# An encoder block on one core: the end of w_out's written TensorE order, and its last T4 product between two banks of transposes

## The chip, the cores and the metric

The kernel runs on one core of one Trainium2 chip. The metric is the device time of one execution in microseconds (us). Before the change the median of three runs is 1320.53 us (1319.11 to 1321.21).

## The reference

One layer of a streaming encoder, 1024 tokens of width 1024, all in float32:

```
def reference(x, norm_mix_pre, norm_mix_post, w_in, b_f, conv_w, w_branch, w_out,
              norm_ffn_pre, norm_ffn_post, w_gate_up, w_down):
    for l in range(DEPTH):
        h = rmsnorm(x, norm_mix_pre[l])
        m = mixer(h, w_in[l], b_f[l], conv_w[l], w_branch[l], w_out[l])
        x = x + rmsnorm(m, norm_mix_post[l])
        h = rmsnorm(x, norm_ffn_pre[l])
        f = swiglu(h, w_gate_up[l], w_down[l])
        x = x + rmsnorm(f, norm_ffn_post[l])
    return x
```

The mixer projects `h` with w_in, runs a gated short convolution and a causal attention with forget gates side by side, takes each through its branch matrix, merges the two under sigmoid gates and multiplies by w_out (1024 x 1024). `swiglu` multiplies by w_gate_up (1024 x 5632), forms silu(g) * u, and multiplies by w_down (2816 x 1024). The change lies at the seam between w_out and gate_up: the last product of the mixer, its norm and residual, the norm before the feed-forward part, and the first products of gate_up.

## The kernel before

**Arithmetic.** Every float32 operand is split into a high and a low part in a reduced float32 type: ScalarE copies the high part (`copy`), VectorE subtracts it (`split`, line 132). A product is three matmuls for each block of the contraction, high x high, high x low, low x high (`mm3`, line 137). The large matrix products use the Strassen-Winograd scheme: seven block products instead of eight, named by their operands, A11, A12, A22, S1 to S4 on one side and B11, B21, B22, T1 to T4 on the other. Here "the T4 product" is A22 with T4. `prod` (line 617) is one block product: four blocks of the contraction, 12 matmuls, into one bank of PSUM.

**w_out.** The 1024 tokens are eight tiles of 128 rows, taken as four pairs (`PAIRS`). For pair i the output has four blocks. The steps, at lines 1656 to 1711, are these. `first` and `second` are A11 and A12. `p_s2` and `p_s1` are S2 and S1. `p_s3` accumulates S3 into the bank that held S2's sum (`b1s[i]`); then ScalarE copies that bank to `c22s[i]` and VectorE adds S1's bank (`b3s[i]`), both raised in priority by `ahead`. `p_s4` accumulates S4 into `b3s[i]`, so it comes after that add; VectorE adds the result to `keeps[i]` and ScalarE squares it for the norm. `p_a22` accumulates the T4 product into `b1s[i]`, so it comes after the copy; ScalarE squares the result. `e_norm(i)` (line 1713) takes the sums of squares of both, scales the pair's two rows of tiles, adds the residual x, stores the sum, squares it, and scales it by the next norm. The first tile of the pair lands in `keeps[i]` (a `raw` buffer of the weights for the first three pairs), the second in `tt`, a tag with one buffer, so the second tile of pair i + 1 waits until that of pair i has been transposed.

**Transposes.** `e_turn(i, tiles)` (line 1740) turns tile 2i + e on TensorE: eight 128 x 128 transposes in two banks of four, q = 0 and 1. The bank q = 0 is copied by ScalarE into rows 0 to 3 of `um`, the bank q = 1 into rows 4 to 7; the copies are raised in priority. `half_split(B11, i)` (line 1796) splits rows 0 to 3 of a pair's columns, `half_split(B21, i)` rows 4 to 7; these are the moving operands of gate_up's A11 and A12 products for the first 512 tokens. `h2_sums(sl)` (line 1800) forms T1 to T4 from tiles sl and 4 + sl: eight subtractions on VectorE and four high parts on ScalarE.

**PSUM.** In this stage pool `pk` has four banks, one for each pair's `b1s` and then for gate_up's first four sums, and pool `psm3` four, for S1/S4 sums (`b3s`), transposes and A12 sums of w_out. From line 1867 on one pool of eight takes their place.

**gate_up's first products.** Before the main loop over blocks of the hidden width, A11 (`f_begin`, line 1774) and A12 (`f_end`, line 1783) of the first eleven blocks are done, as they need only tokens 0 to 511. `f_begin(n)` loads and splits the weights (SyncE's queue, three `raw` buffers, four `hi`, three `lo`), multiplies, and ScalarE copies the sum away; `f_end(n)` accumulates A12 into the same bank, so it waits for that copy. Results go to memory by GpSimd's queue. The first four (`begin_early`, `end_early`) stand between the transposes of pairs 2 and 3, the others follow with `h2_sums`.

**What sets the order.** A planner orders the instructions of each engine by priority (earlier in the program first) and its own costs. An engine named in `strict[0]` is not planned: each instruction is tied behind the one that was written before it on that engine (lines 67 to 82). `pinned(call, name)` (line 119) does this for the instructions of one call. `ahead` raises the priority of a call. Each engine then works off its order strictly: an item that waits holds up all behind it. In this stage `strict[0] = ("tensor",)` holds from line 1814 to line 1862, so TensorE's order is as written; ScalarE's and VectorE's are planned. For the last pair (i = 3) TensorE's written order is: S1, S3, both banks of tile 0 of pair 1, S4, both banks of tile 1 of pair 1, T4; and then `begin_early(0)`, `begin_early(1)`, `end_early(0)`, the transposes of pair 2, and so on.

Of the kernel before, what the change touches and what calls it, by code (L numbers as in the profile page):

```python
# [47 lines left out]
def block_kernel(  # L48
# [18 lines left out]
    strict = [()]  # L67
# [42 lines left out]
    def add(o, a, b):  # L110
        nc.vector.tensor_tensor(o, a, b, op=ALU.add)
# [7 lines left out]
    def pinned(call, *names):  # L119

        was, strict[0] = strict[0], names
        call()
        strict[0] = was

    def ahead(call, by=80):
        with tc.high_priority(offset=by):
            call()

    def copy(o, a):
        nc.scalar.activation(o, a, AF.Copy)  # L130
# [404 lines left out]
    def flat(t):  # L535
        return t.rearrange("p a b -> p (a b)")
# [7 lines left out]
    def raw_t():  # L544
        return wtile("raw", 3)
# [7 lines left out]
    def s4_t():  # L553
        return wtile("s4", 1, F32, (P, 4, P))
# [62 lines left out]
    def prod(ps, w, b, first):  # L617
        (ah, al), (bh, bl) = w, b
        kw = {} if first else dict(skip_group_check=True)
        for k in range(4):  # L620
            mm3(
                ps,
                (ah[:, k, :], al[:, k, :]),
                (bh[:, k, :], bl[:, k, :]),
                first and k == 0,
                k == 3,
                **kw,
            )
# [812 lines left out]
    def x_tile(n, p=None):  # L1441
        if n == 3:
            p, tag = yb_pool, "yb"
        else:
            p, tag = p or wx, f"x{n}"
        return p.tile([P, 2, 4, NC], F32R, tag=tag, name=f"x{n}", bufs=1)

    def both(t):
        return t[:, 0], t[:, 1]
# [183 lines left out]
    def square(src, acc):  # L1633
        junk = ep.tile([P, NC], F32, tag="junk", name="junk")
        nc.scalar.activation(junk, src, AF.Square, accum_out=acc)
# [33 lines left out]
    def rest_ops(i):  # L1669
        a = slice(2 * i * P, (2 * i + 1) * P)  # L1670
        b = slice((2 * i + 1) * P, (2 * i + 2) * P)
        hx, lx = hi_t(), lo_t()
        split(hx[:, LO], lx[:, LO], um[:, LO, a])
        h1, l1 = hi_t(), lo_t()
        split(h1, l1, um[:, :, b])
        split(hx[:, UP], lx[:, UP], s3[i])
        h4, l4 = s4h_t(), s4l_t()
        split(h4, l4, um[:, UP, a])
        return dict(
            S2=(hx[:, LO], lx[:, LO]), S3=(hx[:, UP], lx[:, UP]),  # L1680
            S1=(h1[:, LO], l1[:, LO]), A22=(h1[:, UP], l1[:, UP]),
            S4=(h4, l4),
        )

    def p_s2(i):
        prod(b1s[i], rests[i]["S2"], wob[T2], False)
        copy(keeps[i][:, n2], b1s[i])

    def p_s1(i):
        b3s[i] = bank(psm, "b3")  # L1690
        prod(b3s[i], rests[i]["S1"], wob[T1], True)

    def p_s3(i):
        prod(b1s[i], rests[i]["S3"], wob[T3], False)
        c22s[i] = t_(fe, "c22")

        def keep():
            copy(c22s[i], b1s[i])
            add(c22s[i], c22s[i], b3s[i])

        ahead(keep)
        square(c22s[i], qbs[i][:, 1:2])

    def p_s4(i):
        prod(b3s[i], rests[i]["S4"], wob[B22], False)
        add(keeps[i][:, n2], keeps[i][:, n2], b3s[i])
        square(keeps[i][:, n2], qbs[i][:, 0:1])

    def p_a22(i):
        prod(b1s[i], rests[i]["A22"], wob[T4], False)  # L1710
        square(b1s[i], qas[i][:, 1:2])

    def e_norm(i):
        qa = qas[i]
        add(qa, qa, qbs[i])
        rs = scale2(qa)
        tt = keeps[i], ep.tile([P, D], F32, tag="t", name="tt", bufs=1)
        xp = [xts.popleft() for _ in range(2)]
        ssq = st2("ssq")
        for e, parts in enumerate(  # L1720
            (((slice(0, D), keeps[i]),), ((n1, b1s[i]), (n2, c22s[i])))
        ):
            for ns, c in parts:
                nc.vector.scalar_tensor_tensor(
                    tt[e][:, ns], c, rs[:, e : e + 1], gpo[:, ns], op0=ALU.mult, op1=ALU.mult
                )
            add(xp[e], xp[e], tt[e])
            rows_ = slice((2 * i + e) * P, (2 * i + e + 1) * P)
            nc.gpsimd.dma_start(x2_dram[rows_, :], xp[e])
            nc.scalar.activation(tt[e], xp[e], AF.Square, accum_out=ssq[:, e : e + 1])  # L1730
        rs = scale2(ssq)
        for e in range(2):
            nc.vector.scalar_tensor_tensor(
                tt[e], xp[e], rs[:, e : e + 1], gpr, op0=ALU.mult, op1=ALU.mult
            )
            if 2 * i + 3 + e < ST:
                xts.append(load_xt(2 * i + 3 + e))
        turned.append(tt)

    def e_turn(i, tiles=(0, 1)):  # L1740
        for e in tiles:
            st = 2 * i + e
            ss = slice(st * P, (st + 1) * P)
            for q in range(2):
                tp = psm.tile([P, 4, P], F32, tag="mm", name="tp")

                def turns():
                    for k in range(4):
                        kt = 4 * q + k
                        nc.tensor.transpose(  # L1750
                            tp[:, k, :], turned[i][e][:, kt * P : (kt + 1) * P], ident
                        )

                pinned(turns, "tensor")
                ahead(lambda: copy(um[:, 4 * q : 4 * q + 4, ss], tp))
# [18 lines left out]
    def f_begin(n, b1, p1):  # L1774
        f = FIRSTS[n]
        w, _ = prep_first(f_src(f)[0])
        prod(b1, w["A11"], hb[B11], True)
        pinned(lambda: copy(p1, b1), *(("scalar",) if n >= 8 else ()))
        if f > 1:
            nc.gpsimd.dma_start(pre_dram[f][0], p1)  # L1780
        begun[n] = w, b1, p1

    def f_end(n, c11):
        f = FIRSTS[n]
        w, b1, p1 = begun.pop(n)
        prod(b1, w["A12"], hb[B21], False)
        copy(c11, b1)
        if f > 1:
            nc.gpsimd.dma_start(pre_dram[f][1], c11)
        else:  # L1790
            kept[f] = p1, c11
# [4 lines left out]
    def half_split(b, i):  # L1796
        ss = slice(2 * i * P, (2 * i + 2) * P)
        split(hb[b][0][:, :, ss], hb[b][1][:, :, ss], um[:, (LO, UP)[b], ss])
# [18 lines left out]
    for i in range(PAIRS):  # L1817
        if i + 1 < PAIRS:
            rests.append(rest_ops(i + 1))
        if i:  # L1820
            p_s1(i)
        p_s3(i)
        if i > 1:
            e_turn(i - 2, (0,))
        if i + 1 < PAIRS:
            p_s2(i + 1)
        if i == 3:
            p_s4(i)
        if i > 1:
            e_turn(i - 2, (1,))  # L1830
            half_split(B11, i - 2)
        if i == 2:
            hb.append(both(x_tile(2)))
        if i > 1:
            half_split(B21, i - 2)
        for p_ in ((p_a22, p_s4), (p_s4, p_a22), (p_s4, p_a22), (p_a22,))[i]:
            p_(i)
        e_norm(i)
    hb.append(None)
# [4 lines left out]
    def begin_early(f):  # L1844
        if f == 2:
            raw_t()
        f_begin(f, pk.tile([P, NC], F32, tag="p1", name="b1"), early[f])

    def end_early(f):
        f_end(f, flat(s4_t()))  # L1850

    begin_early(0)
    begin_early(1)
    end_early(0)
    e_turn(2)
    begin_early(2)
    end_early(1)
    begin_early(3)
    end_early(2)
    e_turn(3)  # L1860
    end_early(3)
    strict[0] = ()
    ep_close()
    fe_close()
    psm_close()
# [533 lines left out]
```

## Time and profile before

| | |
|---|---|
| median of 3 runs | 1320.53 us (1319.11 to 1321.21) |
| the profiled execution | 1322.75 us, of which the span from the first to the last instruction is 1321.0 |
| mean granted TensorE clock | 0.997 |
| matmuls, on TensorE | 6776 |
| w_out's first bank of transposes in this stage | starts at 649.17 us |
| gate_up's first product | starts at 675.40 us |

A profile shows one execution. Its page gives busy times by engine and the chain of work that ended last; the views of the trace list, for each engine, the instructions in order of time, merged where they are alike, with the idle time ahead of them in brackets and what ended it. All operations go through helpers, so each has the line 77, and groups are told apart by the names of their tiles: `tp` is a bank of transposes, `raw`, `tt` and `keep` the tiles that they turn, `um` where they land, `x` the operands that `half_split` and `h2_sums` write (and w_out's weights before that), `c` the c22 and c21 tiles, `p` a bank of pool `pk` that w_out uses, `b` any other sum, `s` and `sx` room for gate_up's first results.

### The profile page before, as it was taken

To read this page: it belongs to the slowest core of one execution; us is meant where nothing else is said; L and a number is where in the kernel's file an instruction comes from. 1 tells how busy PE (TensorE), PEld (TensorE's weight loads), DVE (VectorE), ACT (ScalarE), POOL (GpSimd) and SP (SyncE) were. 2 spreads that over 40 slices of the span, in tenths; PEclk is the share of its full clock that TensorE was granted. 3 is DMA by queue.
4 is the path that set the end of the run, shared out by engine and by line. 5 is a ranking of instruction groups with operands and counts; after the bars stand their busy time and mean duration, and the time that the engine had idled before them with its cause. 6 is when DMAs were issued, how large, how long until landed. Compare 5 with 4: busy or idle time off the path is not lost.

```text
span 1321.0 us, 18315 instructions
## 1 busy us (share of the span) xinstructions
PE 1303.3 (99%) x6776; PEld 1089.5 (82%) x6776; DVE 1015.3 (77%) x1595; ACT 583.6 (44%) x935; POOL 154.9 (12%) x289
## 2 busy tenths in 40 slices
PE   9999999999999999999989999999999999999997
PEld 8988888887888888888877888888888888888886
DVE  6975979875656877587888688898888887676685
ACT  6642333253355866445666422323333334444452
POOL 0001100021012212020011012121001110000000
PEclk9999999999999999999999999999999999999999
DMA  6347757778646444499365545563223337966541
GB/s 223 110 117 223 201 155 209 192 212 228 175 144 200 161 145 151 158 344 360 112 214 167 161 160 179 171 200 104 80 96 121 104 106 275 329 254 193 158 167 64
DMA packets 207242, 235.15 MB, mean 178 GB/s; under 512 B 12064, under 2 KB 150368, under 8 KB 207152
## 3 DMA queue, kind: packets, MB, share of 16 engines
q1 hardware_dynamic: 159136, 156.08, 37.5%
q0 software_dynamic: 18832, 63.22, 13.1%
q10 hardware_dynamic: 29184, 14.68, 4.4%
q8 instruction: 53, 0.87, 0.3%
q14 instruction: 37, 0.30, 0.1%
HBM read 161.79 MB, written 72.16 MB: 177 GB/s over the span
## 4 chain that ended last, share of the span: by engine, by line
PE 92%; DVE 3%; DMA 2%; ACT 2%; issue 1%; SPq 0%; POOL 0%; DVEq 0%; ACTq 0%; POOLq 0%
PE b L77 53%; PE pd L77 16%; PE pba L77 3%; PE p L77 3%; PE pv L77 3%; PE tps L77 3%; PE po L77 3%; PE sp L77 2%; PE pbp L77 2%; PE pbv L77 1%; PE zb L77 1%; PE ma L77 1%; PE q L77 1%; PE tp L77 1%; PE mb L77 1%
## 5 line engine op out<-in xcount | busy, mean ns | idle before, releaser
L77 PE MATMUL b<-x,hi 128*128 128x512 f32 x1088 | 338.3, 392 | 4.9 <-ACT c L77 2.9
L77 PEld LDWEIGHTS b<-x,hi 128*128 128x128 f32 x1088 | 204.8, 189 | 48.4 <-ACT c L77 3.3
L77 PE MATMUL b<-x,lo 128*128 128x512 f32 x544 | 213.0, 392 | 0.0
L77 DVE TENSOR_TENSOR lo<-raw,hi 128x1024 fp32r<-128x1024 f32 x90 | 108.3, 1204 | 64.6 <-PE b L77 57.6
L77 ACT ACTIVATE hi<-raw 128x1024 fp32r<-128x1024 f32 (+1 forms) x96 | 97.6, 1018 | 103.7 <-PE b L77 55.2
L77 PEld LDWEIGHTS b<-x,lo 128*128 128x128 f32 x544 | 102.8, 189 | 22.0 <-DVE lo L77 0.3
L77 DVE TENSOR_TENSOR c<-c,b 128x512 f32<-128x512 f32 x138 | 93.7, 680 | 21.6 <-PE b L77 13.4
L77 ACT ACTIVATE hi<-sx 128x1024 fp32r<-128x1024 f32 (+1 forms) x42 | 43.8, 1042 | 125.4 <-PE b L77 116.5
L77 DVE TENSOR_TENSOR lo<-sx,hi 128x1024 fp32r<-128x1024 f32 (+1 forms) x42 | 50.3, 1197 | 25.4 <-PE b L77 22.6
L77 DVE TENSOR_TENSOR sx<-raw 128x512 f32<-128x512 f32 x78 | 53.6, 687 | 20.7 <-DMA raw<-in_w_in_dram 11.1
L77 DVE TENSOR_TENSOR um<-um 128x512 f32<-128x512 f32 x93 | 62.3, 685 | 0.7
L77 PE MATMUL pd<-hi,lo 128*128 128x512 f32 x160 | 62.3, 389 | 0.0
L77 PE MATMUL pd<-hi 128*128 128x512 f32 x160 | 61.9, 390 | 0.0
L77 PE MATMUL pd<-ghi 128*128 128x512 f32 x148 | 57.7, 390 | 0.0
L77 PE MATMUL pd<-glo,ghi 128*128 128x512 f32 x148 | 57.6, 389 | 0.0
L77 PE MATMUL pd<-ghi,glo 128*128 128x512 f32 x148 | 57.6, 389 | 0.0
L77 DVE TENSOR_TENSOR um<-um,b 128x512 f32<-128x512 f32 x68 | 46.0, 682 | 9.5 <-PE b L77 8.5
L77 ACT ACTIVATE sgf<-c 128x512 f32<-128x512 f32 x20 | 12.6, 632 | 91.9 <-DVE c L77 72.8
L77 PE MATMUL b<-hT12h,lo 128*128 128x512 f32 x136 | 53.0, 390 | 0.0
L77 PE MATMUL b<-hT12l,hi 128*128 128x512 f32 x136 | 52.9, 389 | 0.0
L77 PE MATMUL b<-hT34h,hi 128*128 128x512 f32 x136 | 52.9, 389 | 0.0
L77 PE MATMUL b<-hT34l,hi 128*128 128x512 f32 x136 | 52.9, 389 | 0.0
(507 smaller groups left out, 3171.9 us busy)
## 6 DMA issues: line engine op xcount, KB each, us to landing
raw<-in_w_gate_up_dram SPq DMA_DIRECT2D x55, 512.0 KB, 4.0
raw<-in_w_in_dram SPq DMA_DIRECT2D x35, 512.0 KB, 4.4
x<-wo_dram SPq DMA_DIRECT2D x28, 512.0 KB, 7.2
a_dramS<-um POOLq DMA_DIRECT2D x44, 256.0 KB, 2.6
a_dramA<-um POOLq DMA_DIRECT2D x33, 256.0 KB, 2.5
wo_dram<-h ACTq DMA_DIRECT2D x16, 448.0 KB, 4.4
wo_dram<-l ACTq DMA_DIRECT2D x16, 448.0 KB, 6.8
sg<-sg_dram SPq DMA_DIRECT2D x28, 256.0 KB, 3.2
```

The source lines that it names most:

```text
L77: ins = getattr(self.engine, name)(*args, **kw)
```

## The change

Four edits, all of order:

- `e_turn` takes a list of halves, so that one bank can be issued alone.
- In the last pairs the two banks of the second tile are issued apart. For i = 2 they still follow each other. For i = 3 the T4 product (`p_a22`) stands between them, and S4 (`p_s4`), which stood ahead of them, comes last.
- `strict[0] = ()` moves from behind `end_early(3)` to ahead of `begin_early(0)`: gate_up's first products are ordered by the planner. Transposes stay pinned behind whatever is written ahead of them.
- The transposes of pair 2 are written behind `begin_early(0)` (before: behind `end_early(0)`), those of pair 3 behind `begin_early(3)` (before: behind `end_early(2)`).

No instruction is added or removed.

```
-    def e_turn(i, tiles=(0, 1)):
+    def e_turn(i, tiles=(0, 1), halves=(0, 1)):
...
-            for q in range(2):
+            for q in halves:
...
             e_turn(i - 2, (0,))
         if i + 1 < PAIRS:
             p_s2(i + 1)
+        if i > 1:
+            e_turn(i - 2, (1,), (0,))
         if i == 3:
-            p_s4(i)
+            p_a22(i)
         if i > 1:
-            e_turn(i - 2, (1,))
+            e_turn(i - 2, (1,), (1,))
             half_split(B11, i - 2)
...
-        for p_ in ((p_a22, p_s4), (p_s4, p_a22), (p_s4, p_a22), (p_a22,))[i]:
+        for p_ in ((p_a22, p_s4), (p_s4, p_a22), (p_s4, p_a22), (p_s4,))[i]:
             p_(i)
         e_norm(i)
...
+    strict[0] = ()
     begin_early(0)
+    e_turn(2)
     begin_early(1)
     end_early(0)
-    e_turn(2)
     begin_early(2)
     end_early(1)
     begin_early(3)
+    e_turn(3)
     end_early(2)
-    e_turn(3)
     end_early(3)
-    strict[0] = ()
```

More of the change, by code (lines that the diff above doesn't have):

```diff
@@ L1738, in e_norm, with e_turn @@
         turned.append(tt)
-    def e_turn(i, tiles=(0, 1)):
+    def e_turn(i, tiles=(0, 1), halves=(0, 1)):
         for e in tiles:
@@ L1743, in e_turn @@
             ss = slice(st * P, (st + 1) * P)
-            for q in range(2):
+            for q in halves:
                 tp = psm.tile([P, 4, P], F32, tag="mm", name="tp")
@@ L1826, in block_kernel @@
             p_s2(i + 1)
+        if i > 1:
+            e_turn(i - 2, (1,), (0,))
         if i == 3:
-            p_s4(i)
+            p_a22(i)
         if i > 1:
-            e_turn(i - 2, (1,))
+            e_turn(i - 2, (1,), (1,))
             half_split(B11, i - 2)
@@ L1835, in block_kernel @@
             half_split(B21, i - 2)
-        for p_ in ((p_a22, p_s4), (p_s4, p_a22), (p_s4, p_a22), (p_a22,))[i]:
+        for p_ in ((p_a22, p_s4), (p_s4, p_a22), (p_s4, p_a22), (p_s4,))[i]:
             p_(i)
@@ L1850, in end_early @@
         f_end(f, flat(s4_t()))
+    strict[0] = ()
     begin_early(0)
+    e_turn(2)
     begin_early(1)
     end_early(0)
-    e_turn(2)
     begin_early(2)
@@ L1858, in block_kernel @@
     begin_early(3)
+    e_turn(3)
     end_early(2)
-    e_turn(3)
     end_early(3)
-    strict[0] = ()
     ep_close()
```

## The prediction

> **What bounds the kernel now.** I read the page first, then the waits of TensorE, then the timelines of TensorE, ScalarE and VectorE between 640 and 720 us, and last the granted clock by stretch. The page's parts 1 and 4:
>
> ```profile
> PE 1303.3 (99%) x6776; PEld 1089.5 (82%) x6776; DVE 1015.3 (77%) x1595; ACT 583.6 (44%) x935; POOL 154.9 (12%) x289
> ...
> PE 92%; DVE 3%; DMA 2%; ACT 2%; issue 1%; SPq 0%; POOL 0%; DVEq 0%; ACTq 0%; POOLq 0%
> ```
>
> TensorE is the bound. The matmuls are the same after the change, so it can only take away, or add, time in which TensorE waits or runs at a lower clock. Its waits between 590 and 760 us (total, times, longest), and then those from 720 us to the end:
>
> ```profile
> PE b L77 <- ACT c L77: 2.9, 1, 2.9
> PE b L77 <- DVE c L77: 2.3, 1, 2.3
> PE b L77 <- ACT x L77: 0.9, 1, 0.9
> PE b L77 <- DVE x L77: 0.8, 1, 0.8
> ```
>
> ```profile
> PE b L77 <- DVE c L77: 0.4, 1, 0.4
> ```
>
> Behind 720 us there is nearly nothing to wait for, so what is won or lost before that is kept to the end. The four waits are three losses. TensorE's timeline, start and duration, idle time in brackets:
>
> ```profile
> 649.17 1.03 PE L77 MATMUL tp<-ident,raw 128*128 128x128 f32 x8
> 649.96 0.71 PE L77 MATMUL p<-x,hi 128*128 128x512 f32 x2
> ...
> 664.58 1.04 PE L77 MATMUL tp<-ident,raw 128*128 128x128 f32 x8
> 667.89 0.73 PE L77 MATMUL b<-x,s4h 128*128 128x512 f32 x2 [2.27 <-DVE c L77]
> ...
> 671.54 0.71 PE L77 MATMUL p<-x,hi 128*128 128x512 f32 x2
> ...
> 675.40 0.50 PE L77 MATMUL b<-x,hi 128*128 128x512 f32 x1 [0.86 <-ACT x L77]
> 676.66 0.50 PE L77 MATMUL b<-x,hi 128*128 128x512 f32 x1 [0.76 <-DVE x L77]
> ...
> 680.86 0.63 PE L77 MATMUL b<-x,hi 128*128 128x512 f32 x2
> ...
> 708.72 0.39 PE L77 MATMUL b<-x,lo 128*128 128x512 f32 x1
> 712.01 1.22 PE L77 MATMUL b<-x,hi 128*128 128x512 f32 x2 [2.90 <-ACT c L77]
> ...
> 714.74 0.74 PE L77 MATMUL b<-x,hi 128*128 128x512 f32 x2
> ```
>
> A product of 12 matmuls and its price stand in the chain:
>
> ```profile
> 662.02 2.73 PE p L77 x12
> ```
>
> So a product is 2.73 us, 0.227 a matmul, and eight transposes are 0.79 (649.17 to 649.96), a bank of four 0.40. **Loss A:** the transposes of 664.58 leave TensorE free at 665.37; S4 of pair 3 (`p_s4(3)`) starts at 667.89: 2.5 us. **Loss B:** A22·T4 of pair 3 (`p_a22(3)`) starts at 671.54 and leaves TensorE free at 674.27; gate_up's first product should then end at 677.0, and its successor starts at 680.86: 3.9 us. **Loss C:** TensorE is free at 708.95, the next product starts at 712.01 (3.1 us), and its first six matmuls take until 714.74, 2.73 instead of 1.36 (1.4 us): 4.4 us. Together 10.8 us; no version of this change can win more.
>
> The part of B and C that is no waiting is the clock (busy time with counts for PE, PEld, DVE, ACT and POOL, then the clock, DMA share and GB/s):
>
> ```profile
> 668.00:671.00 3.00, 3.00 (x15) 2.46 (x16) 1.03 (x2) 1.75 (x4) 0.54 (x1) 1.00 0.81 254
> ...
> 677.00:680.00 3.00, 3.00 (x9) 2.35 (x8) 2.85 (x12) 2.14 (x7) 0.00 (x0) 0.57 0.08 30
> ...
> 712.00:715.00 3.00, 2.99 (x7) 2.41 (x8) 3.00 (x7) 1.66 (x3) 1.08 (x2) 0.50 0.45 163
> ```
>
> **Part by part: T4 ahead of S4.** Both products accumulate into banks that `p_s3(3)` left. ScalarE copies the first bank, then VectorE adds the second to the copy:
>
> ```profile
> 665.89 0.58 ACT L77 ACTIVATE c<-p 128x512 f32<-128x512 f32 x1
> 666.37 1.07 ACT L77 ACTIVATE um<-tp 128x512 f32<-128x512 f32 x2
> 667.87 0.63 ACT L77 ACTIVATE junk<-c 128x512 f32<-128x512 f32 x1 [0.43 <-DVE c L77]
> ```
>
> ```profile
> 662.75 1.28 DVE L77 SCALAR_TENSOR_TENSOR tt<-xt,r,gpr 128x1024 f32<-128x1024 f32 x1
> ...
> 667.16 0.68 DVE L77 TENSOR_TENSOR c<-c,b 128x512 f32<-128x512 f32 x1
> ```
>
> S4 needs the add (667.84, and it started 0.05 later); A22·T4 needs only the copy (666.47). New order: third bank of transposes 665.37 to 665.77 (the row that it turns, `tt`, stood at 664.0, and of four banks S1's result and two transposes hold three), T4 from 666.52 to 669.25, fourth bank to 669.65 (its bank comes from the copies that end at 667.44), S4 to 672.4. S4's add is then 1.8 us old, so it waits for nothing. Of A, 0.75 us are left (666.52 less 665.77). The upper bound of what is left is A itself, 2.5, if another item slips ahead of the copy on ScalarE; nothing upstream of it is edited, so I take 0.75.
>
> **The third bank early.** Half of the second operand of gate_up's first product is split from rows 0 to 3 of `um`, which the first and third bank fill; the fourth fills rows 4 to 7, which only its A12 product reads. ScalarE and VectorE before:
>
> ```profile
> 671.76 1.06 ACT L77 ACTIVATE hi<-raw 128x1024 fp32r<-128x1024 f32 x1 [1.60 <-DMA raw<-in_w_gate_up_dram]
> 672.72 1.07 ACT L77 ACTIVATE um<-tp 128x512 f32<-128x512 f32 x2
> ...
> 674.29 2.00 ACT L77 ACTIVATE x<-um 128x1024 fp32r<-128x1024 f32 x2
> ```
>
> ```profile
> 671.82 0.75 DVE L77 SCALAR_TENSOR_TENSOR tt<-p,r,gpo 128x512 f32<-128x512 f32 x1 [0.19 <-PE tp L77]
> ...
> 675.38 2.36 DVE L77 TENSOR_TENSOR x<-um,x 128x1024 fp32r<-128x1024 f32 x2 [0.89 <-ACT x L77]
> ```
>
> The rows show what B is: the copies of banks 3 and 4 stand on ScalarE behind a weight split that waits for its DMA until 671.73. With the third bank at 665.77, its copy follows the other two (667.44 to 668.0), the split's high part ends at 669.0 (or 669.9 behind the square of 667.87), the low part, 1.18 on VectorE, by 671.1. The first product can start at 672.4, when S4 ends, without a wait: B goes, 3.9 us. If the copy still stood behind that weight split, B would stay whole. The copy is raised in priority and its bank is due 0.4 us behind its neighbours, while the DMA landed over 5 us behind them, so I take it gone. A and B together: 2.5 - 0.75 + 3.9 = 5.6 us.
>
> **Moved with it.** T4's square (0.63 on ScalarE) comes earlier, S4's add and square 1.7 us later; `e_norm(3)` needs both, and TensorE leaves S4 at 672.4, where it left T4 at 674.3: earlier for it. `e_norm(2)`'s second row waits for the fourth bank (the 0.19 above): 669.9 instead of 671.7. No DMA is issued by what moves, but transposes free `raw` buffers, and the weight loads wait for these; pair 1's first row stays where it was.
>
> **The free order.** The transposes of pairs 2 and 3 stay pinned behind `begin_early(0)` and `begin_early(3)`; the rest of gate_up's first products goes where the planner puts them. The rows of pairs 2 and 3 were ready here, and what made loss C follows:
>
> ```profile
> 681.14 1.28 DVE L77 SCALAR_TENSOR_TENSOR tt<-xt,r,gpr 128x1024 f32<-128x1024 f32 x1
> ...
> 697.98 1.28 DVE L77 SCALAR_TENSOR_TENSOR tt<-xt,r,gpr 128x1024 f32<-128x1024 f32 x1
> ...
> 710.13 0.68 DVE L77 TENSOR_TENSOR sx<-um,sx 128x512 f32<-128x512 f32 x1
> ```
>
> ```profile
> 709.64 0.63 ACT L77 ACTIVATE x<-sx 128x512 fp32r<-128x512 f32 x1 [1.70 <-DVE sx L77]
> ...
> 711.38 0.58 ACT L77 ACTIVATE c<-b 128x512 f32<-128x512 f32 x1
> ```
>
> From `tt<-p` at 671.82 to the end at 682.4 pair 2's second row takes 10.6 us, some 3 of them beside the splits of 675.38 that now go earlier. From 669.9 the row is ready at 678 to 680.5. TensorE passes the first product at 675.1, the second at 677.8, the third at 680.6. Set behind the third, the transposes wait for nothing; behind the second, up to 2.7; behind the first, up to 5.4. I take 1 us, near the second with one row ready. Pair 3 trails pair 2 by 16.8 us before, so it is ready by 697 at the latest, or at about 690 if it follows its transposes as closely as VectorE allows; TensorE gets there between 690.4 (672.4, six products and 1.6 of transposes) and 695.9 (eight). I take nothing more for it.
>
> **Loss C** is the copy of 711.38, queued behind splits that wait for VectorE. The same view from 668 to 709 us:
>
> ```profile
> 668.00:709.00 41.00, 39.38 (x184) 32.14 (x184) 34.17 (x54) 27.82 (x51) 7.04 (x13) 0.96 0.59 204
> ```
>
> VectorE was busy 34.17 of 41.00 us, so with the same work ahead of that place it can win 6.8 at most. TensorE would reach the place at 702.9 (672.4, ten products, 3.2 of transposes), VectorE's chain at 703 (if pair 3 is 9 us earlier, and a part of the work goes behind the copy) to 710 (2 us earlier). C may vanish (4.4 won) or eat up part of the 5.6. I take half of it: 2.2.
>
> Sum: 5.6 - 1.0 + 2.2 = 6.8 us. The profiled execution took 1322.75 (span 1321.0 and 1.75 around it), which gives 1315.95; it lay 2.2 above the median, so from 1320.53: **1313.7 us**.
>
> **A rule of the Trainium skill.** The page on TensorE (TensorE: Matmul & The Clock Gate, Part 1) says that the clock halves after an idle window of about 3.4 us, and its Part 4 that transposes do not count as activity. By that, waits of 0.86 and 0.76 us cost no clock, B would be worth 1.6, the gain 4.5 and the time 1316.0. The trace disagrees on the threshold: 0.57 was granted after these two, while behind A, 3.3 us of transposes and waiting, it was 1.00; the sum keeps the rows.
>
> **Rivals.**
> - *Everything goes* (16%). C vanishes and the transposes wait for nothing: 10.8 - 0.75 = 10.05, 1310.5. For it: the chain of pair 3 starts up to 9 us earlier. Against: VectorE's dense stretch.
> - *VectorE becomes the bound* (10%). The chain gains only 2 us, and the copy of C holds TensorE until 710: 1318.5. For it: 34.17 of 41.00 busy. Against: 6.8 us of idle time that the new order can use, and work that the planner can set behind the copy.
> - *It does not do what it says* (7%). The third bank's copy still stands behind the weight split; the first product starts at 675.4: within 0.5 of 1320.5.
> - *Slower* (10%). The planner counts VectorE too fast: the transposes of pair 2 are set right behind the first product, those of pair 3 right behind `begin_early(3)`. Each waits up to 5.4 us, and each restart costs 1.4 of clock as in C; two such are 13.6, against 5.6 won: up to 1328.5. It decides once the two waits take more than 5.6. For it: C itself shows ScalarE's order built on a VectorE that came later. Against: the row of pair 2 starts 1.8 us earlier, and other products are free to go ahead.
>
> **How the numbers follow.** My forecast has 57%, with 1311.5 (C nearly gone) to 1316.5 (C whole, and more wait at the transposes) as its own range. A measurement of this kernel can tell 0.2%, 2.6 us. Faster by more: 57 + 16 and a hundredth of the VectorE case, 0.74; within: the rest of that case and the one that does nothing, 0.16; slower 0.10. The range goes from the floor (1320.53 - 10.8 = 1309.7) to 1319.5, past the VectorE case; outside are the slower case and the one without effect, 17%.
>
> **What would show it.** Right: T4 of pair 3 starts 0.7 to 0.8 us after the third bank, waiting for ScalarE's `c`; S4 and gate_up's first product follow with no idle time and the granted clock is 1.00 from 668 to 682; the first product starts near 672.4, the third `um<-tp` copy ends near 668. Wrong: a wait of over 2 us of TensorE for `tt` or `keep` at the transposes of pairs 2 or 3, a wait for `x` at 672, or a wait for ScalarE's `c` of 3 us or more around 703 to 710. A stall past 720 us that was not there would break the premise that the rest stays as it is.

## The result, and the profile after

The changed kernel takes 1312.88 us (median of six runs, 1312.38 to 1313.23) against 1320.41 for the kernel before on the same chip (six runs, 1318.72 to 1322.92): a ratio of 0.9942, 95% interval 0.9929 to 0.9955, 7.5 us faster. The forecast was 1313.7. The profiled execution took 1312.85 us, its span 1311.1; against the profiled execution before that is 9.9 us less. The two differences, 7.5 and 9.9, are not the same number, and one experiment below is about that.

TensorE's waits between 590 and 760 us, which were four with 6.8 us in all, are now:

```profile
PE p L77 <- ACT c L77: 0.4, 1, 0.4
PE tp L77 <- DVE keep L77: 0.2, 1, 0.2
PE tp L77 <- DVE raw L77: 0.2, 1, 0.2
```

Its timeline at the end of w_out and at the transposes of pairs 2 and 3:

```profile
664.48 1.04 PE L77 MATMUL tp<-ident,raw 128*128 128x128 f32 x8
665.36 0.60 PE L77 MATMUL tp<-ident,tt 128*128 128x128 f32 x4
666.40 0.73 PE L77 MATMUL p<-x,hi 128*128 128x512 f32 x2 [0.45 <-ACT c L77]
...
669.27 0.60 PE L77 MATMUL tp<-ident,tt 128*128 128x128 f32 x4
669.62 0.71 PE L77 MATMUL b<-x,s4h 128*128 128x512 f32 x2
...
672.47 0.62 PE L77 MATMUL b<-x,hi 128*128 128x512 f32 x2
...
678.01 1.07 PE L77 MATMUL tp<-ident,raw 128*128 128x128 f32 x8 [0.16 <-DVE raw L77]
678.83 0.48 PE L77 MATMUL b<-x,lo 128*128 128x512 f32 x1
679.21 1.06 PE L77 MATMUL tp<-ident,tt 128*128 128x128 f32 x8
...
692.55 1.06 PE L77 MATMUL tp<-ident,keep 128*128 128x128 f32 x8 [0.22 <-DVE keep L77]
693.37 0.48 PE L77 MATMUL b<-x,lo 128*128 128x512 f32 x1
693.74 1.06 PE L77 MATMUL tp<-ident,tt 128*128 128x128 f32 x8
```

Read it from the top: third bank, T4 after a wait of 0.45 us, fourth bank, S4, and gate_up's first product at 672.47 with no idle time ahead of it (before: 675.40). The planner put the first transposes of pair 2 ahead of the last matmul of gate_up's second product, and those of pair 3 inside another product; both meet their rows within 0.2 us. No wait follows at the place of loss C. On ScalarE the copies of the first three banks now run as one group, the split of `x` comes directly behind, and the weight split of the third block stands at 672.46, behind all of them:

```profile
666.25 1.56 ACT L77 ACTIVATE um<-tp 128x512 f32<-128x512 f32 x3
667.85 1.06 ACT L77 ACTIVATE x<-um 128x1024 fp32r<-128x1024 f32 x1
...
671.51 1.06 ACT L77 ACTIVATE x<-um 128x1024 fp32r<-128x1024 f32 x1
672.46 1.05 ACT L77 ACTIVATE hi<-raw 128x1024 fp32r<-128x1024 f32 x1
```

At the place of loss C, ScalarE's copy of gate_up's fifth sum ends at 702.26, ahead of the splits of the third tile's T operands, and TensorE starts the product that accumulates into that bank at 702.82 without a wait:

```profile
701.66 0.60 ACT L77 ACTIVATE c<-b 128x512 f32<-128x512 f32 x1
703.73 0.63 ACT L77 ACTIVATE x<-sx 128x512 fp32r<-128x512 f32 x1 [1.47 <-DVE sx L77]
```

```profile
702.82 0.62 PE L77 MATMUL b<-x,hi 128*128 128x512 f32 x2
```

### The profile page after: what moved, and what is told of

It is laid out like the page before. It is cut to its first block, busy times and chain, and to the rows that moved or that the text cites. A ratio compares the mean times of both kernels' runs of the same rounds, so it can differ in the third digit from the quotient of the medians.

```text
span 1311.1 us, 18310 instructions
## 1 busy us (share of the span) xinstructions
PE 1299.8 (99%) x6776; PEld 1087.3 (83%) x6776; DVE 1015.2 (77%) x1595; ACT 583.5 (45%) x935; POOL 154.9 (12%) x289
## 4 chain that ended last, share of the span: by engine, by line
PE 93%; DVE 2%; ACT 2%; DMA 2%; issue 1%; SPq 0%; DVEq 0%; ACTq 0%
PE b L77 54%; PE pd L77 16%; PE pba L77 3%; PE pv L77 3%; PE tps L77 3%; PE po L77 3%; PE sp L77 2%; PE p L77 2%; PE pbp L77 2%; PE pbv L77 1%; PE zb L77 1%; PE ma L77 1%; PE q L77 1%; PE tp L77 1%; PE mb L77 1%
## 5 line engine op out<-in xcount | busy, mean ns | idle before, releaser
L77 PE MATMUL b<-hT34h,lo 128*128 128x512 f32 x136 | 53.0, 389 | 0.0
```

The costliest lines, as they stand in the source:

```text
L77: ins = getattr(self.engine, name)(*args, **kw)
```

## The experiments

All but one are medians of five to seven executions, beside the kernel before. They fall into three groups: the median of before was 1321.33 us beside `e1_wout_only`, `e2_turns_only`, `e3_third_bank_late` and `e5_turns_strict`, 1321.63 beside `e6_third_bank_only`, `e10_splits_behind` and `e7_both_banks_first`, and 1321.58 beside the last three below. Where a run is set against the changed kernel, it is the 1313.04 us that this one took in the last group, so differences of a few tenths mean nothing. "L" below is the tail that the change rewrote: from `begin_early(0)` to `strict[0] = ()`.

**The end of w_out alone** (`e1_wout_only`): the changed kernel with L as before.

```
-    strict[0] = ()
     begin_early(0)
-    e_turn(2)
     begin_early(1)
     end_early(0)
+    e_turn(2)
...
     end_early(3)
+    strict[0] = ()
```

> Only the end of w_out as in the change (third bank, T4, fourth bank, S4); the transposes of pairs 2 and 3 and the written order of gate_up's first products as before. Theory: losses A and B go by this alone (wait before T4 about 0.45, the first product at 672.5), and C goes too, because everything on VectorE comes some 6 us earlier: 9 to 10 us in the profile, median within 1 us of the changed kernel (1312 to 1314). Rival: C needs the moved transposes or the free order; then TensorE waits 3 to 4 us for ScalarE's copy around 703 to 707 and the median is 1315 to 1317.

1313.03 us, ratio 0.9936 (0.9923 to 0.9949). The whole gain is there. Its profile has two waits, before T4 and at the place of loss C:

```profile
665.35 0.73 PE L77 MATMUL p<-x,hi 128*128 128x512 f32 x2 [0.49 <-ACT c L77]
...
702.82 0.73 PE L77 MATMUL b<-x,hi 128*128 128x512 f32 x2 [0.51 <-ACT c L77]
```

C shrank from 2.9 to 0.5 us without any edit at it. The expected time holds and the rival falls, but the reason that was given for C does not hold. VectorE does come earlier, by 6.4 us (the first split of the third tile's T operands runs at 703.23, before at 709.64); but TensorE comes as much earlier, free at 702.15 against 708.95. What changed is the place of the awaited copy on ScalarE: before, it stood behind 11 splits of T operands, three of them the third tile's; here it stands behind 8, ahead of the third tile's:

```profile
702.18 0.58 ACT L77 ACTIVATE c<-b 128x512 f32<-128x512 f32 x1
703.23 0.63 ACT L77 ACTIVATE x<-sx 128x512 fp32r<-128x512 f32 x1 [0.47 <-DVE sx L77]
```

The changed kernel has the same 8. Why the planner chose this order here is not shown.

**The other half alone** (`e2_turns_only`): the kernel before with the new L.

> Only the other half of the change: free order of gate_up's first products and the transposes of pairs 2 and 3 written earlier; the end of w_out as before. Theory: A (2.3 us wait for VectorE's add) and B (the first product held until 675.4 and at a lower clock) stay whole, as nothing of them is touched, and C stays for the most part: 0 to 2 us faster than before. Rival, that the free order is what wins: B or C is filled by other products, 4 us or more faster, and the profile shows less than 1 us of waiting behind 677 us.

1317.24 us, ratio 0.9965 (0.9953 to 0.9977): 4.1 us faster, against 0 to 2 expected. The rival was right on the time and nearly on the waits: it named less than 1 us behind 677 us, and there are 1.3. Its timeline:

```profile
664.62 1.04 PE L77 MATMUL tp<-ident,raw 128*128 128x128 f32 x8
667.82 0.73 PE L77 MATMUL b<-x,s4h 128*128 128x512 f32 x2 [2.17 <-DVE c L77]
...
675.91 0.84 PE L77 MATMUL b<-x,hi 128*128 128x512 f32 x3
677.21 0.50 PE L77 MATMUL b<-x,hi 128*128 128x512 f32 x1 [0.46 <-DVE x L77]
...
695.94 1.06 PE L77 MATMUL tp<-ident,keep 128*128 128x128 f32 x8 [0.63 <-DVE keep L77]
...
708.89 0.72 PE L77 MATMUL b<-x,hi 128*128 128x512 f32 x2 [0.22 <-ACT c L77]
```

A is untouched. While the low part of `x` is missing, three first matmuls (high x high) of three products run at 675.91, which the written order did not allow, and the wait of C is down to 0.2. The copy of C still stands behind 10 splits here, but the third tile's come 2.5 us earlier than before and TensorE only 0.4 (708.51 against 708.95). So the free order does work when there is something to fill; behind the new end of w_out there is nothing.

**The third bank late** (`e3_third_bank_late`): the changed kernel, with

```
-        if i > 1:
-            e_turn(i - 2, (1,), (0,))
         if i == 3:
             p_a22(i)
         if i > 1:
-            e_turn(i - 2, (1,), (1,))
+            e_turn(i - 2, (1,))
```

> The changed kernel, with the third bank of transposes behind T4, beside the fourth. Theory: A stays away (T4 starts some 0.4 us earlier, as no bank stands ahead of it, and waits that much longer for the copy), but the split for gate_up's first product starts only when both banks are copied, about 672, so that the first product waits 1 to 2 us at 672.8 for x, and maybe for some lower clock: 1 to 3 us slower than the changed kernel. Rival: the place of the third bank is worth nothing, since S4 hides the copy and the split anyway: within 0.5 us of the changed kernel.

1313.53 us, ratio 0.9938 (0.9926 to 0.995), some 0.5 us above the changed kernel and not to be told from it. Its waits:

```profile
PE p L77 <- ACT c L77: 0.7, 1, 0.7
PE b L77 <- DVE x L77: 0.5, 1, 0.5
PE b L77 <- ACT x L77: 0.2, 1, 0.2
```

The first product does wait for `x`: 0.7 us idle, 1.1 counted from start to start, at the lower edge of the 1 to 2 expected, and the clock stays at 1.00 from 664 to 682 us. The expected 1 to 3 us of time are not there. On ScalarE the copies of both banks (670.40) stand ahead of the weight split (675.33), and S4 covers most of the rest.

**The third bank early, S4 first** (`e6_third_bank_only`): the kernel before, with the list of halves in `e_turn` and

```
+        if i > 1:
+            e_turn(i - 2, (1,), (0,))
         if i == 3:
             p_s4(i)
         if i > 1:
-            e_turn(i - 2, (1,))
+            e_turn(i - 2, (1,), (1,))
```

> The kernel before with one edit: the third bank of transposes stands ahead of S4, the fourth behind it, T4 last; everything else as before. Theory: A stays at about 2.1 us (S4 waits for the add, with one bank more in the wait), B goes, because the split for gate_up's first product is then done beside S4 and T4; VectorE is some 4 us earlier for pair 2, so C shrinks: 4 to 7 us faster than before. Rival, after the run with the third bank late: the third bank's place is worth little and it is the order T4, S4 that removes B; then the first product still waits 1 us or more for x, and this is at most 2 us faster than before.

1317.76 us, ratio 0.9971 (0.9961 to 0.9982): 3.9 us faster, just short of the theory's 4 to 7 and outside the rival's 2. Its waits:

```profile
PE b L77 <- ACT c L77: 2.5, 1, 2.5
PE b L77 <- DVE c L77: 1.7, 1, 1.7
```

No wait for `x` is left: this bank's place alone takes B away. A keeps 1.7 and C 2.5 us. Together with the run before: either edit takes B away, or all but 0.7 us of it, and each covers for the other. C tells something as well. The third tile's splits come 4.9 us earlier than before, TensorE comes 4.4 earlier, and the copy stands behind 11 splits as before:

```profile
704.79 0.63 ACT L77 ACTIVATE x<-sx 128x512 fp32r<-128x512 f32 x1 [1.71 <-DVE sx L77]
...
706.53 0.58 ACT L77 ACTIVATE c<-b 128x512 f32<-128x512 f32 x1
```

So an earlier VectorE alone left most of C in place.

**The splits tied** (`e10_splits_behind`): the kernel before, with this in `h2_sums`:

```
-            split(hb[o][0][:, :, a], hb[o][1][:, :, a], t)
+            pinned(lambda: split(hb[o][0][:, :, a], hb[o][1][:, :, a], t), "scalar")
```

> The kernel before, with ScalarE's splits of the T operands tied behind what is written ahead of them on ScalarE, so that the copies of gate_up's fifth and sixth sums no longer stand behind splits that wait for VectorE; TensorE's order is as before. Theory: C is only this place in ScalarE's queue: A and B stay, the wait of 2.9 us for ScalarE's copy and the low clock behind it go, 3 to 4.4 us faster than before. Rival: VectorE as a whole is the bound there, and the wait comes back at once in another form (for a low part, or for T operands at the main loop): within 1.5 us of before.

1316.61 us, ratio 0.9963 (0.995 to 0.9977), 5.0 us faster, more than the 3 to 4.4 expected. Its waits, and the stretch from 686 to 709 us, first of the profile before, then of this run (time, busy time of PE, PEld, DVE, ACT and POOL, clock, DMA share, GB/s):

```profile
PE b L77 <- DVE c L77: 2.2, 1, 2.2
PE b L77 <- DVE x L77: 0.9, 1, 0.9
```

```profile
686.00:709.00 23.00, 23.00 (x119) 19.25 (x117) 20.25 (x31) 17.48 (x31) 4.00 (x8) 1.00 0.61 209
```

```profile
686.00:709.00 23.00, 23.00 (x117) 19.42 (x116) 15.15 (x23) 15.93 (x29) 4.83 (x9) 1.00 0.75 242
```

C is gone, A and B are there. VectorE does 15.15 us of work in this stretch instead of 20.25, the rest later, and no wait comes back up to the end of the kernel. So C was not VectorE's capacity: it was the place of one copy in ScalarE's queue. In this profile the clock fell behind A (0.57 from 668 to 672 us), as in the second profile of before below; against that one it is 3.7 us shorter (1316.51 against 1320.21), near the 3.1 us of C. What else is in the 5.0 stays open.

**The transposes at once** (`e5_turns_strict`): the changed kernel, with `strict[0] = ()` back at the end of L, so that the transposes of pair 2 follow the first product directly.

> The changed kernel, but TensorE's order stays as written until the end of the first products, so the transposes of pair 2 stand right behind gate_up's first product and those of pair 3 right behind the fourth. Theory: this is the wait that the free order takes away: pair 2's rows are ready at about 677.9 and 679.1, TensorE gets there at 675.2, so it waits 2.5 to 4 us for raw and tt, and part of it comes back as a lower clock; at pair 3 it waits at most 2 us: 3 to 6 us slower than the changed kernel. Rival: VectorE gains as much from the early transposes as TensorE loses: within 1 us of the changed kernel.

1316.5 us, ratio 0.9962 (0.995 to 0.9974), 3.5 us above the changed kernel. TensorE's timeline and a stretch behind it:

```profile
678.20 1.12 PE L77 MATMUL tp<-ident,raw 128*128 128x128 f32 x8 [2.64 <-DVE raw L77]
679.40 1.94 PE L77 MATMUL tp<-ident,tt 128*128 128x128 f32 x8
```

```profile
680.00:682.00 2.00, 2.00 (x10) 1.81 (x9) 1.86 (x2) 1.19 (x2) 0.00 (x0) 0.50 0.96 291
```

This is the mechanism of the slower rival, brought about by the edit: a wait of 2.6 us and then half the clock. It is smaller than the rival's 5.4 for one pair, and pair 3 waits for nothing.

**Both banks ahead of T4** (`e7_both_banks_first`): the changed kernel with `e_turn(i - 2, (1,))` ahead of `p_a22(i)` and nothing behind it.

> The changed kernel with the fourth bank of transposes beside the third, ahead of T4. Theory: it finds no free bank until ScalarE has copied the first, at about 666.8, so TensorE waits 1 us for that and T4 starts 0.8 later; S4 hides the rest: 0.3 to 0.8 us slower than the changed kernel. Rival: the bank is free or the wait for the copy of c is as long anyway: no difference.

1314.15 us, ratio 0.9942 (0.9929 to 0.9954). The wait for a bank is there:

```profile
PE b L77 <- ACT c L77: 1.3, 1, 1.3
PE tp L77 <- ACT um L77: 0.7, 1, 0.7
```

It costs little: from the first bank of transposes (663.59) to gate_up's first product (671.75) it takes 8.16 us, against 7.99 in the changed kernel, so 0.2 and not the 0.3 to 0.8 expected. The kernel lies 1.1 us above the changed one; its other wait, of 1.3 us, stands at the place of C, where the copy is behind 10 splits in this planner's order and not 8.

**Before, once more** (`e0_before_again`, one execution).

> The kernel before once more, for a second profile. If the 9.9 us between the two profiles against 7.5 between the medians comes from the clock, this profile shows the same three waits (2.3, 1.6, 2.9 us) with a lower clock at other or fewer places, and its time follows the sum of the low-clock stretches; if it comes from the waits, they differ by 2 us or so.

1320.21 us, 2.5 less than the first profiled execution. Its waits stand at the same three places: 2.2, 0.9 (expected 1.6) and 3.1 us. Three stretches, first of the profile before, then of this one:

```profile
668.00:674.30 6.30, 6.30 (x32) 5.15 (x32) 4.11 (x5) 4.29 (x10) 0.54 (x1) 1.00 0.84 280
674.30:682.00 7.70, 6.08 (x19) 4.43 (x18) 6.66 (x15) 5.44 (x12) 0.54 (x1) 0.78 0.34 119
709.00:715.00 6.00, 3.10 (x8) 2.41 (x8) 6.00 (x12) 3.98 (x7) 1.08 (x2) 0.72 0.62 197
```

```profile
668.00:674.30 6.30, 6.30 (x25) 5.02 (x25) 2.52 (x4) 4.10 (x8) 0.54 (x1) 0.73 0.78 257
674.30:682.00 7.70, 6.80 (x30) 5.28 (x29) 7.63 (x16) 5.67 (x12) 1.13 (x3) 1.00 0.32 113
709.00:715.00 6.00, 3.88 (x17) 3.23 (x18) 6.00 (x11) 4.63 (x9) 1.08 (x2) 1.00 0.56 191
```

In the first profile the clock fell behind the waits B and C and not behind A; in the second behind A alone, where it cost less, since TensorE would have waited for `x` at B anyway. By the sixth matmul behind C the second execution is 2.1 us ahead, which is this; a wait of 0.4 us behind 720 us, which only the first profile has, makes up the 2.5 between the two.

**The changed kernel beside two others** (`after_again`, `e1b_wout_only`, `e12_after_splits_behind`; the last is the changed kernel with the edit of `e10_splits_behind`).

> The changed kernel once more, beside the two others on the same chip: waits of 0.4, 0.2 and 0.2 us and a granted clock of 1.00 through the stage, 7 to 9 us faster than before; several runs within 1 us of each other, as there is no restart at which the clock could fall.

> The end of w_out alone, now beside the changed kernel. Theory: the free order and the earlier transposes have nothing left to take, so the two agree within 0.8 us (a wait of 0.5 us for ScalarE's copy near 703 here, two of 0.2 us at the transposes there). Rival: they are worth 1 us or more on top.

> The changed kernel with ScalarE's splits of the T operands tied as in the run that removed loss C alone. Theory: C is gone already, so nothing is left to win: within 0.8 us of the changed kernel. Rival: VectorE's chain is still what ends last behind 695 us, and the tie wins 1 us or more; or the T operands come late to the main loop and it loses as much.

In this order: 1313.04 us, ratio 0.9934 (0.9921 to 0.9946); 1313.26, 0.9935 (0.9923 to 0.9948); 1312.56, 0.993 (0.9917 to 0.9944). The three agree within 0.7 us and none can be called faster. The stretch from 668 to 710 us, of the changed kernel and of the one with the tied splits:

```profile
668.00:710.00 42.00, 41.66 (x201) 34.16 (x200) 40.65 (x65) 32.30 (x59) 8.14 (x15) 1.00 0.70 235
```

```profile
668.00:710.00 42.00, 41.84 (x203) 34.75 (x202) 33.73 (x53) 29.21 (x54) 8.85 (x17) 1.00 0.71 231
```

TensorE is all but full in both. VectorE has 40.65 or 33.73 us of work in the same stretch, and the time is the same.

## Why the prediction was right, and where it was not

- **A.** Forecast: T4 at 666.52 with 0.75 us left. Measured: 666.40, a wait of 0.45 (0.2 in the second profile); counted from the end of the bank, as the forecast counted, 0.64. Right, for the reason given: T4 needs the copy, S4 the add.
- **B.** Forecast: the first product at 672.4 with no wait. Measured: 672.47 with none, and 1.00 granted. The size is right; the reason is too narrow. The third bank's early place is sufficient (`e6_third_bank_only`) but not necessary for most of it (`e3_third_bank_late`, with 0.7 us left): with T4 ahead and gate_up's products free, the copies come before the weight split also when both banks stand behind T4, and S4 is there to cover the split of `x`.
- **The free order.** Forecast: 1.0 us of new waits at the transposes. Measured: 0.16 and 0.22. The planner broke a product open for them. `e5_turns_strict` shows what the forecast feared: 3.5 us in the median. But the free order only repairs what the earlier transposes would cost: `e1_wout_only`, with both left as before, is as fast.
- **C.** Forecast: half of 4.4 us, because VectorE was taken for the bound. This is the step that was mis-sized: all of it went. TensorE came to the place at 702.82 (forecast 702.9), and the awaited copy ended at 702.26, just ahead of the 703 to 710 of the forecast. An earlier VectorE alone does not give that: the third tile's splits start at 703.73, and behind three of them, as before the change, the copy would have started near 705.5 by ScalarE's rows, some 3 us too late (an estimate). It went because the copy stands behind 8 splits instead of 11. `e10_splits_behind` shows that this place decides: the copy stood behind splits that it does not need, and VectorE had room; `e6_third_bank_only`, with an earlier VectorE and the old place, kept 2.5 us. "With the same work ahead of that place it can win 6.8 at most" was the wrong limit, as the work need not stand ahead of that place. The forecast named this way out ("a part of the work goes behind the copy") and gave it half, without a row that spoke for it; why the planner takes it is not shown here.
- **From the profile to the median.** Forecast: 6.8 of a loss of 10.8 us, taken off the median of 1320.53. But 10.8 was the loss of one execution, whose clock fell twice where it hurt; the second profile of before lost 2.5 us less. In the profiles the floor is met (1322.75 - 10.8 + the 0.8 us of waits that are left = 1312.75; measured 1312.85), in the medians 7.5 us were won. That the forecast of 6.8 came within 1 us of 7.5 is in part luck: C was put 2.2 too small and the transposes 0.6 too dear, and the profiled execution, from which the losses were read, lay 2.3 us above the median.
- **The halves of the change overlap.** One half alone wins 8.3 us, the other alone 4.1, both together no more than the first (`after_again` beside `e1b_wout_only`). The prediction added terms as if each edit had its own loss; B and C each had two cures.
- **The rule of the Trainium skill** (TensorE: Matmul & The Clock Gate, Part 1). That the clock falls only after an idle window of about 3.4 us is not what these runs show. Waits of 2.46 us (`e6_third_bank_only`) and 2.90 us (the profile before), both with whole products right ahead of them, were followed by a granted clock of 0.50 over the next 3 us, and in the profile before two of 0.86 and 0.76 by 0.57; a wait of 3.09 us in the second profile of before was followed by 1.00. So the forecast was right to keep the rows. (The 1316.0 that was worked out for the rule kept the 1.4 us of clock in C, which by the rule would have gone as well.) The same page's remark that this window runs freely fits the finding that the same wait A cost clock in one execution and none in another; the window itself is not visible in these runs.

## What to carry to other kernels

When an engine with work for all of its time still waits, look at what stands ahead of the awaited item in the queue of the engine that makes it: here a copy waited behind a weight split that waited for a DMA, and another behind splits that nobody needed yet. That VectorE was busy for 34 of 41 us did not make it the bound. Between two products that need different results of the same step, put the one first whose operand is ready first, and let the other cover what follows. Before terms read in one profile are taken off a median, take a second profile: losses of clock behind short waits move from run to run, and two edits that cure the same loss don't add.

## What the runs showed of the hardware that was not expected

The granted clock fell to about half behind some waits of 0.8 to 2.9 us and not behind others, one of 3.1 us among them, and which ones it was changed between executions of the same program: behind A it was 1.00 in the first profile of before and 0.73 (668 to 674.3 us) in the second.

This shows in the times, though it is not all of their spread. Of the 31 executions of before beside the experiments, the 14 with a mean clock of 0.996 averaged 1322.3 us, the 16 with 0.997 averaged 1321.0, and one with 0.998 took 1319.63. The changed kernel, with no wait over 0.5 us in this stage, ran at 0.998 and 0.999, and its eleven executions lay within 1.1 us. But the end of w_out alone (`e1b_wout_only`), with the same clocks and no wait over 0.7 us, ran from 1311.75 to 1314.59 us in five; where that spread comes from is not shown.
